# Order and layout of the q/k weight parts, the place of the Fourier channel products, and the last squares, in an encoder block

## The chip, the cores and the metric

The kernel runs on one core of a Trainium2 chip. The metric is the device time of one execution in microseconds (us), as the median of several runs. TensorE (PE) multiplies, VectorE (DVE) and ScalarE (ACT) work elementwise, GpSimd (POOL) does small elementwise steps, and DMA queues issued by SyncE (SP) and GpSimd bring the weights in.

## What is computed

One layer of an encoder on 256 positions of 2048 features. A combined projection gives q (12 heads of 128), k and v (4 heads each) and u (512 columns). Attention runs within a window of 128 positions; u goes through a two-dimensional Fourier transform, by groups of 128 channels, and a linear map for each group. Both results are normed, concatenated and projected; a gated feed-forward part with a short convolution and a final norm follow.

```python
def reference(x, norm1_g, w_in, sink, w_fourier, attn_out_g, fourier_out_g, w_out,
              norm2_g, w_up, dw_w, dw_b, w_down, normf_g):
    for _ in range(DEPTH):
        h = _rmsnorm(x, norm1_g)
        proj = h @ w_in
        ...
        a = _rmsnorm(_window_attention(q, k, v, sink), attn_out_g)
        f = _rmsnorm(_fourier_mix(u, w_fourier), fourier_out_g)
        x = x + jnp.concatenate([a, f], axis=-1) @ w_out
        x = x + _conv_ffn(_rmsnorm(x, norm2_g), w_up, dw_w, dw_b, w_down)
    return _rmsnorm(x, normf_g)

def _fourier_mix(u, w_fourier):
    B, S = u.shape[0], u.shape[1]
    ug = u.reshape(B, S, N_FOURIER_GROUPS, FOURIER_GROUP_DIM).astype(jnp.float32)
    f = jnp.real(jnp.fft.fft2(ug, axes=(1, 3), norm='ortho'))
    y = jnp.einsum('bsgc,gcd->bsgd', f.astype(u.dtype), w_fourier)
    return y.reshape(B, S, FOURIER_WIDTH)
```

## The kernel before

**Units and parts.** The work up to the output projection is a row of units, numbered by slot. Each unit has one weight tile of 128 x 2048 float32 numbers (1 MB), loaded by one DMA. Slots 4 to 7 are v, slots 8 to 23 the sixteen q and k heads in the order k0, q0, q1, q2, k1, q3 and so on, slots 24 to 31 the output projection. TensorE multiplies in a float32 format of less precision, so `split` (L168) makes two parts of each weight tile: ScalarE copies the raw tile into the high part (L174), and VectorE subtracts that from the raw tile for the low part (L175). A q/k unit is sixteen products of a high part with 512 columns (the high and the low half of the activations side by side, L362) and sixteen of a low part with 256 columns (L364). `still_weights` (L351) sets their order: with `lag` 0 a high and a low product alternate from the start, with `lag` 4 five high ones come first and five low ones last. `OPENING` (L49) gives lag 4 to the four k heads and to q1, q7 and q10; all others have 0. `parts_tile` (L156) hands out one of three buffers and places the high part at column 0 of it and the low part 16 columns past its middle ("still" in `PLACES`, L154).

**Order.** Nothing is scheduled by the framework: every engine runs its instructions in the order in which the program issues them. `unit` (L402) runs for slot i first the list `before[i]` (on TensorE, in front of the unit's products), then the products, then `beside[i]`, then `step`, which splits the weights of slot i + 2 and issues the load for slot i + 5, then `behind[i]`. `step` comes after `beside`, so on VectorE the low part of slot i + 2 stands behind the posts of slot i.

**A head's path.** With s the slot of a q head: the sum of its two halves and its own parts (`qk_out`, `qk_parts`) are issued beside s + 1, its scores on TensorE ahead of s + 2, `scores_out` on VectorE beside s + 2 (it adds the distances and finds the maxima, and writes the tile `sc`), `exps` on ScalarE behind s + 2, `weigh` on VectorE beside s + 3, the transposes of `sc` on TensorE (`turn`) ahead of s + 4, `turn_out` (the parts `pt`) beside s + 4, and the products with v (`values`) ahead of s + 5, with `values_out` beside it.

**The Fourier path.** `fourier_rows` and `fourier_rows_out` (slot 7) leave four tiles `uf0` to `uf3`. They carry the tag `sc`, as the score tiles do, and the tag has four buffers. `fourier_channels` (L547) multiplies `uf` of one group by the group's map, as full float32 products, ahead of slots 9 to 12. `fourier_channels_copy` (ScalarE, beside the same slot), `fourier_channels_join` (VectorE, behind it) and `fourier_channels_out` (beside the next slot) follow. The squares' total over the four groups (`total`) runs ahead of slot 14, its scale beside it. The buffers of a tag are given to a new tile when the last reader of an older one is through; the waits for that are put in with the build.

**The end.** The last columns of the down-projection, 512 for each of four column groups and two row blocks, come out in `last_product` (L1220). `last_post` (L1100) adds them to the residual on VectorE and squares the sum on ScalarE, with the row total in `ssq3`. The very last group, (3, 1), comes in two halves of 256 columns. `most_of` and `last_scale` (L1105, L1113) put the totals together on VectorE, GpSimd takes the power -0.5, and `finish` scales and stores the four column groups.

Of the kernel before, what the change touches and what calls it, by code (L numbers as in the profile page):

```python
# [8 lines left out]
F32 = mybir.dt.float32  # L9
F32R = mybir.dt.float32r  # L10
AF = mybir.ActivationFunctionType
ALU = mybir.AluOpType

P = 128
D = 2048
S = 256
NK = D // P
HD = 128
NH = 12
NKV = 4  # L20
GQA = 3
NG = 4
AW = NH * HD
FW = NG * P
DFF = 5504
NF = DFF // P
EPS = 1e-6
# [17 lines left out]
QK_ORDER = []  # L45
for _g in range(NKV):
    QK_ORDER += [("k", _g)] + [("q", _g * GQA + _i) for _i in range(GQA)]

OPENING = {("q", 1): 4, ("q", 7): 4, ("q", 10): 4}  # L49
OPENING.update({("k", g): 4 for g in range(NKV)})  # L50
N_U, N_V, N_QK = 0, 4, 8
N_OUT = N_QK + len(QK_ORDER)

# [43 lines left out]
def block_kernel(  # L97
# [18 lines left out]
    nc = tc.nc  # L116
    SL = slopes()
    ctx.enter_context(tc.manual_schedule())
    base = ctx.enter_context(tc.tile_pool(name="base", bufs=1))
    wp = ctx.enter_context(tc.tile_pool(name="wp", bufs=1))  # L120
# [4 lines left out]
    def f32(ap):  # L125
        return ap.bitcast(F32)
# [4 lines left out]


    units = [(None, 2048, "first")] * N_V
    units += [(w_in[i - N_V], 2048, "first" if i < N_QK else "still") for i in range(N_V, 24)]
    units += [(w_out[i], 2048, "moving") for i in range(16)]
    n_front = len(units)
    items, up_index = ff_items(), {}
# [17 lines left out]

    def parts_tile(name, place):  # L156
        t = wp.tile([P, 2 * 2048 + 128], F32R, tag="parts", name=name, bufs=3)
        oh, ol = PLACES[place]
        return t[:, oh : oh + 2048], t[:, 2048 + ol : 4096 + ol]

    def load(i):

        if i < len(units) - 1 and i not in raws:
            src, n, _ = units[i]
            raws[i] = wp.tile([P, 2048], F32, tag="raw", name=f"raw{i}", bufs=RAW)
            nc.sync.dma_start(raws[i][:, 0:n], src)

    def split(i):  # L168
        if i >= len(units):
            return  # L170
        _, n, place = units[i]
        raw = raws[i][:, 0:n]
        hi, lo = (t[:, 0:n] for t in parts_tile(f"parts{i}", place))
        nc.scalar.activation(hi, raw, AF.Copy)  # L174
        nc.vector.tensor_tensor(lo, raw, f32(hi), ALU.subtract)  # L175
        halves[i] = hi, lo
        load(i + RAW)
        load_more(i + RAW)
# [16 lines left out]
    xs = [base.tile([P, 2, 512], F32, tag=f"xs{c}", name=f"xs{c}") for c in range(4)]  # L195
# [10 lines left out]
    half_pow = base.tile([P, 2], F32, tag="half_pow", name="half_pow")  # L206
# [4 lines left out]
    ps = bank(dn, "ps_warm")  # L211
# [11 lines left out]
    for c in range(4):  # L223
        t = base.tile([P, 4, 512], F32R, tag=f"hT{c}", name=f"hT{c}")
# [36 lines left out]
    k = 0  # L261
# [89 lines left out]
    def still_weights(hi, lo, ps, kk, lag=0):  # L351


        todo = [("hi", k) for k in kk[: lag + 1]]
        for n, k in enumerate(kk):
            todo.append(("lo", k))
            todo += [("hi", q) for q in kk[lag + 1 + n : lag + 2 + n]]
        for part, k in todo:
            h = hT[k // 4][:, k % 4, :]
            s = slice(k * P, (k + 1) * P)  # L360
            if part == "hi":
                nc.tensor.matmul(ps, hi[:, s], h, start=k == 0, stop=False)  # L362
            else:
                nc.tensor.matmul(  # L364
                    ps[:, 0:S], lo[:, s], h[:, 0:S], start=False, stop=k == NK - 1
                )

    def still_thirds(hi, lo, ps):
# [24 lines left out]
    before, beside, behind = {}, {}, {}  # L393

    def at(when, i, f, *a):
        when.setdefault(i, []).append((f, a))
# [188 lines left out]
    at(beside, 8, lambda: rows_out(v_hi, v_lo, ps_v))  # L585
    at(behind, 8, distances)

    def fourier_channels_steps():
        for g in range(NG):
            i = 9 + g  # L590
            at(beside, i, fourier_channels_copy, g)
            at(behind, i, fourier_channels_join, g)
            at(beside, i + 1, fourier_channels_out, g)
        at(beside, 14, total_scale, "f", FW)


    ps_v = [bank(mm, f"ps_v{b}") for b in range(2)]
# [124 lines left out]
    for i in range(N_QK, N_OUT + 8):  # L722
        heads = {i - s: h for (kind, h), s in slot_of.items() if kind == "q"}
        new = [kh for kh, s in slot_of.items() if i - s == 1]
        if i - 9 in range(NG):
            at(before, i, fourier_channels, i - 9)
        if 5 in heads:
            at(before, i, values, heads[5])
        if 4 in heads:
            at(before, i, turn, heads[4])  # L730
        if i == 14:
            at(before, i, total, sq_f, "f")
        if 2 in heads:
            at(before, i, scores, heads[2])
        if 3 in heads:
            at(beside, i, weigh, heads[3])
        for kind, h in new:
            at(beside, i, lambda k=kind, h=h: qk_out(k, h, st.pop(("ps", k, h))))
        if 5 in heads:
            at(beside, i, values_out, heads[5])  # L740
        if 4 in heads:
            at(beside, i, turn_out, heads[4])
        for kind, h in new:
            at(beside, i, qk_parts, kind, h)
        if 2 in heads:
            at(beside, i, scores_out, heads[2])
            at(behind, i, exps, heads[2])

    fourier_channels_steps()
    for n, (kind, h) in enumerate(QK_ORDER):  # L750

        def work(hi, lo):
            ps = st["ps", kind, h] = bank(mm, f"ps_{kind}{h}")
            still_weights(hi, lo, ps, range(NK), lag=OPENING.get((kind, h), 0))

        unit(N_QK + n, work)

# [49 lines left out]
    for n, (c, kq) in enumerate(OUT_ORDER):  # L807
        i = N_OUT + n
# [14 lines left out]
        if kq >= 2:  # L823
            part = "a" if kq == 2 else "f"
            ps = ps_a[c] if kq < 3 else ps_a[c, "f"]
# [18 lines left out]
    parts = {}  # L844
# [242 lines left out]
    ssq3 = base.tile([P, 2, 5], F32, tag="ssq3", name="ssq3")  # L1087

    def square_sum(c, b, part, o, n):
        junk = wp.tile([P, 512], F32, tag="junk", name=f"junkc{c}{b}{part}")  # L1090
        nc.scalar.activation(
            junk[:, 0:n], xs[c][:, b, o : o + n], AF.Square,
            accum_out=ssq3[:, b, part : part + 1],
        )
# [5 lines left out]
    def last_post(c, b, ps, o=0, n=512, part=None):  # L1100

        add_scaled(xs[c][:, b, o : o + n], ps, b)
        square_sum(c, b, c if part is None else part, o, n)

    def most_of(b, n):  # L1105

        tot = base.tile([P, 1], F32, tag=f"tot3{b}", name=f"tot3{b}")
        nc.vector.tensor_reduce(tot, ssq3[:, b, 0:n], mybir.AxisListType.X, ALU.add)
        var = base.tile([P, 1], F32, tag=f"part3{b}", name=f"part3{b}")
        nc.vector.tensor_scalar(var, tot, 1.0 / D, EPS, ALU.mult, ALU.add)  # L1110
        return var

    def last_scale(b, n, var):  # L1113
        v = base.tile([P, 1], F32, tag=f"var3{b}", name=f"var3{b}")
        nc.vector.scalar_tensor_tensor(
            v, ssq3[:, b, n : n + 1], 1.0 / D, var, ALU.mult, ALU.add
        )
        r = base.tile([P, 1], F32, tag=f"rstd3{b}", name=f"rstd3{b}")
        nc.gpsimd.tensor_tensor(r, v, half_pow[:, 0:1], ALU.pow)
        return r  # L1120
# [17 lines left out]
    for q in range(2):  # L1138
        kind, j = items[q]
        ps = bank(mm, f"ps_{kind}{j}")  # L1140
# [16 lines left out]
    for n, it in enumerate(items):  # L1157
# [8 lines left out]
        if it[0] in ("gate", "val"):  # L1166
            kind, j = it
            ps = bank(mm, f"ps_{kind}{j}")
# [39 lines left out]
    i = up_index[n]  # L1208
# [11 lines left out]
    def last_product(c, b, o=0, n=512, part=None):  # L1220
        hi, lo = halves[i + c]
        ps = bank(dn, f"ps_e{c}{b}{o}")[:, 0:n]
        for q, k in enumerate(LAST):
            w = slice(q * 512 + o, q * 512 + o + n)
            ah, al = (act[k][:, p * S + b * P : p * S + (b + 1) * P] for p in range(2))
            end = q == len(LAST) - 1
            nc.tensor.matmul(ps, ah, hi[:, w], start=q == 0, stop=False)
            nc.tensor.matmul(ps, al, hi[:, w], start=False, stop=False)
            nc.tensor.matmul(ps, ah, lo[:, w], start=False, stop=end)
        if (c, b) == (0, 0):  # L1230
            ff_step(items.index(("last", 0)))
            split_last(3)
        last_post(c, b, ps, o, n, part)
        if c < 3:
            gain(c, b)
# [3 lines left out]
    r3 = last_scale(0, 3, most_of(0, 3))  # L1239
# [5 lines left out]
    for _ in outs:  # L1245
        pass
    last_product(2, 1)
    for p in range(2):
        last_product(3, 1, p * 256, 256, 3 + p)
    r3 = last_scale(1, 4, most_of(1, 4))  # L1250
    for _ in finish(1, r3, (2, 0, 3, 1)):
        pass

# [104 lines left out]
```

## Time and profile before

| | us |
|---|---|
| median of 3 runs | 946.41 |
| the runs | 946.23 to 946.63 |
| the profiled execution | 945.75 |
| its span | 944.0 |

The span is the time from the first to the last instruction of the program. The rows are read thus: in the time-ordered view, start, length, engine, line, operation, tiles and shapes, and in brackets the idle time of the engine before the row and what ended it. A row may hold several like instructions (x5); its length is then that of the group. A matmul's end is modelled and overlaps the next one's start, so the pace of TensorE is read from start to start. In the chain of waits a row has start, length, engine, tile, line and count. In the table of windows each engine has its busy time and, in brackets, its instructions; the number behind POOL's is the granted TensorE clock.

### The profile page before, as it was taken

To read this page: it belongs to the slowest core of one execution; us is meant where nothing else is said; L and a number is where in the kernel's file an instruction comes from. 1 tells how busy PE (TensorE), PEld (TensorE's weight loads), DVE (VectorE), ACT (ScalarE), POOL (GpSimd) and SP (SyncE) were. 2 spreads that over 40 slices of the span, in tenths; PEclk is the share of its full clock that TensorE was granted. 3 is DMA by queue.
4 is the path that set the end of the run, shared out by engine and by line. 5 is a ranking of instruction groups with operands and counts; after the bars stand their busy time and mean duration, and the time that the engine had idled before them with its cause. 6 is when DMAs were issued, how large, how long until landed. Compare 5 with 4: busy or idle time off the path is not lost.

```text
span 944.0 us, 15017 instructions
## 1 busy us (share of the span) xinstructions
PE 934.7 (99%) x6275; PEld 857.6 (91%) x6275; DVE 711.1 (75%) x817; ACT 536.6 (57%) x624; POOL 48.2 (5%) x64
## 2 busy tenths in 40 slices
PE   9999999999999999999999999999999999999996
PEld 8889998888888999999999999999999999999985
DVE  7568877666667766869776887768878678889695
ACT  7656766554454645446555565555555555655544
POOL 0000000000000000000000000000000000000003
PEclk9999999999999999999999999999999999999999
DMA  9864544456558677677798778787787978779742
GB/s 361 312 224 137 176 140 173 134 179 202 195 223 271 220 232 238 188 241 238 250 261 257 243 238 274 249 264 228 261 242 238 298 249 256 248 217 265 222 176 89
DMA packets 32628, 215.00 MB, mean 228 GB/s; under 512 B 3600, under 2 KB 3856, under 8 KB 8240
## 3 DMA queue, kind: packets, MB, share of 16 engines
q1 hardware_dynamic: 28448, 184.55, 53.7%
q0 software_dynamic: 4112, 29.49, 16.5%
q8 instruction: 49, 0.80, 0.3%
q14 instruction: 19, 0.16, 0.0%
HBM read 211.93 MB, written 2.10 MB: 227 GB/s over the span
## 4 chain that ended last, share of the span: by engine, by line
PE 99%; POOL 0%; ACT 0%; issue 0%; DVE 0%; ACTq 0%; POOLq 0%
PE ps_val L375 22%; PE ps_gate L375 21%; PE ps_q L362 5%; PE ps_P L1081 3%; PE ps_P L1080 3%; PE ps_P L1079 3%; PE ps_N L1080 3%; PE ps_N L1081 3%; PE ps_N L1079 3%; PE ps_q L364 2%; PE ps_u L257 2%; PE ps_a L347 2%; PE ps_a L345 2%; PE ps_a L346 2%; PE ps_gate L362 2%; PE ps_val L362 2%
## 5 line engine op out<-in xcount | busy, mean ns | idle before, releaser
L175 DVE TENSOR_TENSOR parts<-raw,parts 128x2048 fp32r<-128x2048 f32 (+1 forms) x129 | 293.5, 2275 | 72.9 <-ACT parts L174 72.8
L174 ACT ACTIVATE parts<-raw 128x2048 fp32r<-128x2048 f32 (+1 forms) x129 | 245.9, 1906 | 82.2 <-PE ps_gate L375 19.9
L375 PEld LDWEIGHTS ps_val<-hU,parts 128*128 128x128 f32 x1824 | 211.6, 188 | 2.2
L375 PE MATMUL ps_val<-hU,parts 128*128 128x256 f32 x1824 | 212.9, 276 | 0.0
L375 PEld LDWEIGHTS ps_gate<-hU,parts 128*128 128x128 f32 x1776 | 206.4, 188 | 2.5
L375 PE MATMUL ps_gate<-hU,parts 128*128 128x256 f32 x1776 | 207.3, 276 | 0.0
L362 PE MATMUL ps_q<-hT,parts 128*128 128x512 f32 x192 | 66.0, 395 | 0.0
L856 ACT ACTIVATE fa_v<-ps_val 128x256 f32<-128x256 f32 x38 | 14.6, 384 | 88.3 <-PE ps_val L375 88.2
L966 DVE TENSOR_TENSOR parts_N<-sumw,parts_N 128x2048 fp32r<-128x2048 f32 x18 | 41.2, 2291 | 21.2 <-ACT parts_N L965 21.1
L1079 PE MATMUL ps_P<-parts_P,op_P 128*128 128x512 f32 x144 | 56.0, 389 | 0.0
L1080 PE MATMUL ps_P<-parts_P,op_P 128*128 128x512 f32 x144 | 56.0, 389 | 0.0
L1081 PE MATMUL ps_P<-parts_P,op_P 128*128 128x512 f32 x144 | 56.0, 389 | 0.0
L364 PE MATMUL ps_q<-hT,parts 128*128 128x256 f32 x192 | 51.6, 279 | 0.0
L362 PEld LDWEIGHTS ps_q<-hT,parts 128*128 128x128 f32 x192 | 35.9, 188 | 7.4
L965 ACT ACTIVATE parts_N<-sumw 128x2048 fp32r<-128x2048 f32 x18 | 34.4, 1914 | 14.3 <-PE ps_gate L375 10.6
L1079 PE MATMUL ps_N<-parts_N,op_N 128*128 128x512 f32 x108 | 42.0, 389 | 0.0
L1080 PE MATMUL ps_N<-parts_N,op_N 128*128 128x512 f32 x108 | 42.0, 389 | 0.0
L1081 PE MATMUL ps_N<-parts_N,op_N 128*128 128x512 f32 x108 | 42.0, 389 | 0.0
L345 PE MATMUL ps_a<-parts,cat 128*128 128x512 f32 x96 | 37.9, 395 | 0.0
L347 PE MATMUL ps_a<-parts,cat 128*128 128x512 f32 x96 | 37.5, 391 | 0.0
L346 PE MATMUL ps_a<-parts,cat 128*128 128x512 f32 x96 | 37.3, 389 | 0.0
L364 PEld LDWEIGHTS ps_q<-hT,parts 128*128 128x128 f32 x192 | 35.4, 188 | 0.3
(350 smaller groups left out, 1513.1 us busy)
## 6 DMA issues: line engine op xcount, KB each, us to landing
raw<-in_w_up SPq DMA_DIRECT2D x86, 1024.0 KB, 5.6
raw<-in_w_in SPq DMA_DIRECT2D x20, 1024.0 KB, 6.4
sumw<-in_w_down POOLq DMA_DIRECT2D x18, 1024.0 KB, 8.5
raw<-in_w_out SPq DMA_DIRECT2D x16, 1024.0 KB, 4.8
raw<-in_w_down_late SPq DMA_DIRECT2D x4, 1024.0 KB, 6.2
u_raw<-in_u_in SPq DMA_DIRECT2D x5, 768.0 KB, 10.8
raw<-in_w_down_last SPq DMA_DIRECT2D x4, 768.0 KB, 4.4
xs<-in_x SPq DMA_DIRECT2D x4, 512.0 KB, 15.3
```

What stands on the lines that cost most here:

```text
L174: nc.scalar.activation(hi, raw, AF.Copy)
L175: nc.vector.tensor_tensor(lo, raw, f32(hi), ALU.subtract)
L345: nc.tensor.matmul(ps, ah, wh, start=first and q == q0, stop=False)
L346: nc.tensor.matmul(ps, al, wh, start=False, stop=False)
L347: nc.tensor.matmul(ps, ah, wl, start=False, stop=last and q == q0 + len(kk) - 1)
L362: nc.tensor.matmul(ps, hi[:, s], h, start=k == 0, stop=False)
L364: nc.tensor.matmul(ps[:, 0:S], lo[:, s], h[:, 0:S], start=False, stop=k == NK - 1)
L375: nc.tensor.matmul(ps[:, 0:S], w[:, s], h[:, o : o + S], start=k == 0 and n == 0, stop=k == NK - 1 and n == 2,)
L966: nc.vector.tensor_tensor(lo, src, f32(hi), ALU.subtract)
L1079: nc.tensor.matmul(ps, o[:, 0, p, :], hi[:, s], start=first and p == 0, stop=False)
L1080: nc.tensor.matmul(ps, o[:, 1, p, :], hi[:, s], start=False, stop=False)
L1081: nc.tensor.matmul(ps, o[:, 0, p, :], lo[:, s], start=False, stop=end)
```

## The change

Three things. First, every q/k unit has lag 7: eight high products, then eight times a low and a high one, then eight low ones. Its parts lie in four pieces of 1024 columns, the high ones at columns 16 and 1088 of the buffer and the low ones at 2128 and 3168; ScalarE's copy and VectorE's subtraction write them with one instruction each, as before. Second, the Fourier channel products of groups 0 to 3 stand ahead of slots 13, 14, 15 and 17, behind `values` and in front of `turn`; the squares' total and its scale move from slot 14 to slot 19. Third, the squares of the last 512 columns of the second row block are taken on VectorE with one multiplying reduction for each half; ScalarE adds up the other three totals with a scaled copy, and GpSimd's power reads the finished sum.

```diff
-OPENING = {("q", 1): 4, ("q", 7): 4, ("q", 10): 4}
-OPENING.update({("k", g): 4 for g in range(NKV)})
...
+        if place == "qk":
+
+            return [
+                t[:, o : o + 2 * n].rearrange("p (h f) -> p h f", h=2)[:, :, 0:1024]
+                for o, n in ((16, 1072), (2128, 1040))
+            ]
...
-        hi, lo = (t[:, 0:n] for t in parts_tile(f"parts{i}", place))
+        hi, lo = parts_tile(f"parts{i}", place)
+        if place == "qk":
+            raw = raw.rearrange("p (h f) -> p h f", h=2)
+        else:
+            hi, lo = hi[:, 0:n], lo[:, 0:n]
         nc.scalar.activation(hi, raw, AF.Copy)
         nc.vector.tensor_tensor(lo, raw, f32(hi), ALU.subtract)
...
+    CHANNELS_AT = (13, 14, 15, 17)
+
     def fourier_channels_steps():
-        for g in range(NG):
-            i = 9 + g
+        for g, i in enumerate(CHANNELS_AT):
             at(beside, i, fourier_channels_copy, g)
             at(behind, i, fourier_channels_join, g)
             at(beside, i + 1, fourier_channels_out, g)
-        at(beside, 14, total_scale, "f", FW)
+        at(beside, 19, total_scale, "f", FW)
...
-        if i - 9 in range(NG):
-            at(before, i, fourier_channels, i - 9)
         if 5 in heads:
             at(before, i, values, heads[5])
+        if i in CHANNELS_AT:
+            at(before, i, fourier_channels, CHANNELS_AT.index(i))
         if 4 in heads:
             at(before, i, turn, heads[4])
-        if i == 14:
+        if i == 19:
             at(before, i, total, sq_f, "f")
...
-            still_weights(hi, lo, ps, range(NK), lag=OPENING.get((kind, h), 0))
+            still_weights(hi, lo, ps, range(NK), lag=7)
...
-        square_sum(c, b, c if part is None else part, o, n)
+        if (c, b) != (3, 1):
+            square_sum(c, b, c if part is None else part, o, n)
...
+    sums3 = base.tile([P, 12], F32, tag="sums31", name="sums31")
+    most = base.tile([P, 3], F32, tag="most31", name="most31")
+    nc.scalar.activation(
+        most, ssq3[:, 1, 0:3], AF.Copy, scale=1.0 / D, accum_out=sums3[:, 0:1]
+    )
+    squares = wp.tile([P, 512], F32, tag="junk", name="junkc31")
     for p in range(2):
-        last_product(3, 1, p * 256, 256, 3 + p)
-    r3 = last_scale(1, 4, most_of(1, 4))
+        last_product(3, 1, p * 256, 256)
+        y = xs[3][:, 1, p * 256 : (p + 1) * 256]
+        nc.vector.tensor_tensor_reduce(
+            squares[:, p * 256 : (p + 1) * 256], y, y, 1.0 / D,
+            sums3[:, 0:1] if p else EPS, ALU.mult, ALU.add, sums3[:, p + 1 : p + 2],
+        )
+        if p == 0:
+            nc.vector.tensor_tensor(sums3[:, 0:1], sums3[:, 0:1], sums3[:, 1:2], ALU.add)
+    r3 = base.tile([P, 1], F32, tag="rstd31", name="rstd31")
+    nc.gpsimd.tensor_tensor(r3, sums3[:, 2:3], half_pow[:, 0:1], ALU.pow)
```

More of the change, by code (lines that the diff above doesn't have):

```diff
@@ L133, in block_kernel @@
     units = [(None, 2048, "first")] * N_V
-    units += [(w_in[i - N_V], 2048, "first" if i < N_QK else "still") for i in range(N_V, 24)]
+    units += [(w_in[i - N_V], 2048, "first" if i < N_QK else "qk") for i in range(N_V, 24)]
     units += [(w_out[i], 2048, "moving") for i in range(16)]
@@ L359, in still_weights @@
             h = hT[k // 4][:, k % 4, :]
-            s = slice(k * P, (k + 1) * P)
+            w = hi if part == "hi" else lo
+            if len(w.shape) == 3:
+                w = w[:, k // 8, k % 8 * P : (k % 8 + 1) * P]
+            else:
+                w = w[:, k * P : (k + 1) * P]
             if part == "hi":
-                nc.tensor.matmul(ps, hi[:, s], h, start=k == 0, stop=False)
+                nc.tensor.matmul(ps, w, h, start=k == 0, stop=False)
             else:
                 nc.tensor.matmul(
-                    ps[:, 0:S], lo[:, s], h[:, 0:S], start=False, stop=k == NK - 1
+                    ps[:, 0:S], w, h[:, 0:S], start=False, stop=k == NK - 1
                 )
```

## The prediction

> **What bounds the kernel now.** I read the page's busy table first, then its chain of waits, then the windows of the stretch that the change touches, then the time-ordered view of each engine there.
>
> ```profile
> PE 934.7 (99%) x6275; PEld 857.6 (91%) x6275; DVE 711.1 (75%) x817; ACT 536.6 (57%) x624; POOL 48.2 (5%) x64
> ...
> PE 99%; POOL 0%; ACT 0%; issue 0%; DVE 0%; ACTq 0%; POOLq 0%
> ...
> 53.19:162.09 108.90, 108.90 (x689) 98.27 (x688) 84.80 (x191) 71.83 (x139) 8.12 (x11) 1.00 0.48 163
> ```
>
> The last row is the stretch from the first q/k unit to the first product of the output projection: TensorE is busy for all of its 108.90 us, at full granted clock. So nobody keeps it waiting there, and only two things can move the end: a shorter stream of products, or a wait that appears. VectorE is busy for 84.80 us of the 108.90, ScalarE for 71.83; the slack is what covers their waits now.
>
> How long is the stream? In the chain of waits the small groups between the units have one length each, and the units differ:
>
> ```profile
> 58.10 0.76 PE L364 MATMUL ps_k<-hT,parts 128*128 128x256 f32 x5
> 58.69 0.60 PE L550 MATMUL ps_y<-uf,G 128*128 128x129 f32 x4
> 59.05 0.48 PE L362 MATMUL ps_q<-hT,parts 128*128 128x512 f32 x1
> 59.37 0.28 PE L364 MATMUL ps_q<-hT,parts 128*128 128x256 f32 x1
> ...
> 64.74 0.60 PE L550 MATMUL ps_y<-uf,G 128*128 128x129 f32 x4
> 65.10 1.41 PE L362 MATMUL ps_q<-hT,parts 128*128 128x512 f32 x5
> 66.34 0.28 PE L364 MATMUL ps_q<-hT,parts 128*128 128x256 f32 x1
> 66.46 0.39 PE L362 MATMUL ps_q<-hT,parts 128*128 128x512 f32 x1
> 66.68 0.28 PE L364 MATMUL ps_q<-hT,parts 128*128 128x256 f32 x1
> ...
> 84.23 0.44 PE ps_t L687 x4
> 84.67 0.71 PE ps_s L637 x6
> 90.83 0.71 PE ps_o L709 x6
> 91.98 0.34 PE ps_totf L485 x4
> ...
> 320.91 5.44 PE ps_val L375 x48
> ```
>
> The first q unit takes 64.74 - 59.05 = 5.69 us. The same number of columns in the feed-forward takes 5.44 (last row), the best pace this trace has. In the stretch stand eleven score groups and nine value groups of 0.71, nine transposes and four Fourier products of 0.44, and one total of 0.34: 20.3 us. That leaves 108.90 - 20.3 = 88.6 for sixteen units, 1.5 over 16 x 5.44 = 87.04.
>
> **The change, part by part.**
>
> *Eight high parts first, parts in four pieces.* The products are the same; only their order and the addresses of the weights change. ScalarE's copy and VectorE's subtraction keep 2048 elements each. From the rows: five low products in a row take (58.69 - 58.10) / 5 = 0.118 each, a pair of high and low at its better pace 66.68 - 66.34 = 0.34. A high product behind a Fourier group takes 59.37 - 59.05 = 0.32, where 66.68 - 66.46 = 0.22 is usual, so 0.1 belongs to the start; the run of five from 65.10 to 66.34 is then 0.23 each. Eight high, eight pairs and eight low in the old layout would be 8 x 0.23 + 8 x 0.34 + 8 x 0.118 = 5.50, and sixteen of them 88.1: a gain of 0.5. If the new offsets bring the pace of 5.44, the gain is 1.5. If instead every pair ran at the slow pace of the first q unit (5.69 less 0.1 for its start, over 16, is 0.35), a unit would be about 5.60 and the loss 1.0. No row shows these offsets, so the ends are -1.5 and +1.0; I take -0.7, nearer to the old layout's own rows than to the best pace, which only other shapes reach.
>
> *Fourier products beside transposes.* On TensorE nothing is gained to speak of: a Fourier group is 0.44 wherever it stands, and the slow first product behind it (those 0.32 for 0.22) is mostly the end of the group itself. I take 0, with 0.1 either way. The cost is elsewhere. The Fourier rows (`uf`, L547 to L550 read them) live in the four buffers of the tag `sc`, in which the scores' tiles live too. Before, product g stood at slots 9 to 12, so all were free when the scores needed them. Now they are read at slots 13, 14, 15 and 17. In the order of the changed program, with its waits, the first write of `sc0` on VectorE (slot 11) waits for the semaphore count that Fourier product 0 gives at the head of slot 13; `sc1` for the transposes of `sc0` in that same slot, since they share a buffer; `sc2` (slot 13) for product 1 at the head of slot 14. Queued behind `sc0` on VectorE are the low part of unit 13, the weighing of head 0, and the sum and low part of q2. TensorE needs head 0's weighed scores for the transposes that stand directly behind product 0, and q2 for the scores behind those. So everything between the two has lost its cover:
>
> ```profile
> 73.52 0.42 DVE L653 CUSTOM_DVE_ANT_0 sc<-ps_s,rel 128x256 f32<-128x256 f32 x1
> ...
> 74.88 0.48 DVE L218 SCALAR_TENSOR_TENSOR cat<-y,vec,cat 128x256 fp32r<-128x256 f32 x1
> 75.96 2.29 DVE L175 TENSOR_TENSOR parts<-raw,parts 128x2048 fp32r<-128x2048 f32 x1 [0.61 <-ACT parts L174]
> 78.17 0.28 DVE L563 TENSOR_TENSOR y<-yh 128x127 f32<-128x127 f32 x1
> ...
> 78.64 0.15 DVE L676 TENSOR_TENSOR sm<-sm,ex 128x2 f32<-128x2 f32 x1
> ...
> 79.56 0.42 DVE L616 TENSOR_TENSOR add_q<-ps_q,tmp_q 128x256 f32<-128x256 f32 x1
> 80.47 0.42 DVE L218 SCALAR_TENSOR_TENSOR qT<-add_q,qT 128x256 fp32r<-128x256 f32 x1 [0.48 <-ACT qT L217]
> ...
> 94.20 0.48 DVE L218 SCALAR_TENSOR_TENSOR cat<-ps_o,vec,cat 128x256 fp32r<-128x256 f32 x1
> 95.62 0.69 DVE L700 TENSOR_TENSOR pt<-ps_t,pt 128x512 fp32r<-128x512 f32 x1 [0.94 <-ACT pt L699]
> ```
>
> In slot 13, from the end of product 0: scores and their maxima 74.88 - 73.52 = 1.36; the low part 78.17 - 75.96 = 2.21 (ScalarE's exponentials run beside it); weighing 79.56 - 78.64 = 0.92; with 0.1 for the handovers TensorE idles 4.6. Then q2's sum and low part, 80.47 + 0.42 - 79.56 = 1.33, of which the transposes cover 0.44: 0.8 more with its handover. Slot 13 costs 5.4.
>
> What is late next: `sc2` starts at product 1, and behind it on VectorE, before the values of head 1 can run at the head of slot 15, stand 1.36, the low part 2.21, the join of Fourier group 0 (78.64 - 78.17 = 0.47), weighing 0.92, a sum 0.34, and from the `cat` part to the end of `pt` 95.62 + 0.69 - 94.20 = 2.11, in which ScalarE's square, waiting for that `cat`, holds its `pt` copy back. That is 7.4 against the transposes and one unit, 0.44 + 5.44 = 5.9 on TensorE: a stall of 1.5 at slot 15. The same list stands before the values of head 4 at slot 19, where the join of group 3 and a late `sc5` meet: 1.5 again. Slot 18 has it without the join, half covered: 0.6, an estimate from the same rows. From slot 20 no Fourier work is left and the covers of before return. Sum: 5.4 + 1.5 + 0.6 + 1.5 = 9.0; ends 5.4 (only the first) and 12 (each slot from 15 to 19 late by about a square's wait more).
>
> The moved steps issue no DMA; each slot's 1 MB load goes out after its low part, three units ahead, and a later TensorE only gives it more time. POOL's additions of the Fourier squares stay off the path, and the scale of the Fourier half, moved from slot 14 to 19, is first used in the output projection, past slot 24. TensorE's half-speed start is a rival below.
>
> *The last squares on VectorE.*
>
> ```profile
> 935.01 0.18 ACT L1091 ACTIVATION_READ_ACCUMULATOR junkc<-xs 128x1 f32 x1
> ...
> 935.72 0.48 DVE L865 SCALAR_TENSOR_TENSOR xs<-ps_e,rstd,xs 128x256 f32<-128x256 f32 x1 [0.55 <-PE ps_e L1229]
> ...
> 936.30 0.42 ACT L1091 ACTIVATE junkc<-xs 128x256 f32<-128x256 f32 x1 [0.52 <-DVE tot L1108]
> 936.62 0.19 ACT L1091 ACTIVATION_READ_ACCUMULATOR junkc<-xs 128x1 f32 x1
> 936.84 0.16 DVE L1115 SCALAR_TENSOR_TENSOR var<-ssq,part 128x1 f32<-128x1 f32 x1 [0.38 <-ACT junkc L1091]
> 937.08 0.55 POOL L1119 TENSOR_TENSOR rstd<-var,half_pow 128x1 f32<-128x1 f32 x1 [0.53 <-DVE var L1115]
> ```
>
> Now the sum ends at 935.72 + 0.48 = 936.20 and the power starts at 937.08. After: a reduction of 256 columns like L653 (0.42) and its accumulator, then one handover to POOL of 0.08: 936.8, a gain of 0.3. But VectorE must first add ScalarE's total of the other three columns, issued after the square that ends at 935.19 and itself an accumulating ScalarE step (at most the 0.42 and 0.19 of the rows above), and the sum of the last half stands behind it: up to 0.2 back. I take -0.2, ends -0.3 and +0.1.
>
> **The sum.** The profiled execution took 945.75 (span 944.0 and 1.75 around it), 0.66 below the median of 946.41. 945.75 - 0.7 + 0 + 9.0 - 0.2 = 953.85; with the 0.66, 954.5 as a median.
>
> **The rivals.**
>
> *TensorE falls back to its starting speed.* At the head of the span:
>
> ```profile
> 0.99 4.37 PE L213 MATMUL ps_warm<-ones 128*128 128x128 f32 x20 [0.99 <-POOL ones L205]
> ```
>
> Twenty passes of 128 columns in 4.37 us are 0.22 each; four in a transpose group take 0.44, 0.11 each. So TensorE starts at half speed and stays there some four microseconds. If the 4.6 us of idling in slot 13 bring that back, about 4.2 us run at half speed: +2.1, 956.6. Against it: this trace has no second gap to show it. The Trainium skill, "TensorE: Matmul & The Clock Gate", Part 1, says that a whole idle window of about 3.4 us halves the clock and that the windows run freely; the half-speed start agrees with it, and by it a gap of 4.6 would hold such a window about one time in three.
>
> *Only the first stall costs.* If the later slots keep their covers, 3.6 less: 950.9. For it: VectorE has 24 us idle in the 108.90. Against it: the list of slot 15 is longer than the unit beside it.
>
> *The layout goes the wrong way.* Units of 5.60: 1.7 more than in the sum, 956.2. For it: the pairs change pace from unit to unit already.
>
> *The other side: the wait is hidden.* In the trace, `sc0` is weighed at 79.56, 4.7 us before its transposes at 84.23. If the buffers came free early enough for that lead to cover the wait, only the gains would be left: 946.41 - 1.5 - 0.2 = 944.7, faster. It decides if product 0 ends five microseconds ahead of the transposes; it stands directly before them, so this needs the changed program to wait otherwise than its semaphores say.
>
> **How the numbers follow.** Forecast 0.60, half speed 0.20, first stall only 0.10, layout 0.05, hidden 0.05. The forecast's own range is 951.5 to 957 (the ends of the stall partly used). The range of all is 950.2 to 958.5. What a measurement can tell from no change is 0.2%, 1.9 us. Faster 0.04, same 0.02, slower 0.94: the hidden wait gives the first two, all else is slower by over 4 us.
>
> **What would show it.** Right: TensorE idle for 4 to 5 us between the first Fourier product and the first transposes, ended by VectorE's weighing; then about 1.5 before the values of head 1; no waits from slot 20 on; units of 5.4 to 5.5; the last power about 0.6 us after the last sum of the residual instead of 0.88. Wrong: no idle TensorE in slot 13, or idle time in the unit products themselves, which would make the low parts or the loads the cause; or a granted clock under 1.00 behind the gap, which would be the half-speed rival.

## The result, and the profile after

| | before | after |
|---|---|---|
| median | 946.48 us (4 runs) | 957.86 us (4 runs, 956.86 to 958.09) |
| profiled execution | 945.75 | 958.08 |
| its span | 944.0 | 956.3 |
| first q/k unit starts at | 53.19 | 53.42 |
| first product of the output projection at | 162.09 | 173.37 |

After over before is 1.0118, with a 95% interval from 1.0106 to 1.0130: slower. The two stretches of the span after the first unit's start hold nearly all of the 12.3 us: 173.37 - 53.42 = 119.95 against 108.90, and from there to the end 956.3 - 173.37 = 782.93 against 944.0 - 162.09 = 781.91.

The table of windows of the changed kernel, first for the stretch from the first unit to the output projection, then for four windows of 3.4 us around the moved Fourier product. The columns are the window, its length, each engine's busy time, the granted clock, the DMA share and GB/s:

```profile
53.42:173.37 119.95, 113.57 (x689) 100.89 (x688) 83.42 (x190) 70.20 (x139) 10.41 (x11) 0.97 0.43 147
...
82.87:86.28 3.41, 0.06 (x1) 0.00 (x0) 3.25 (x7) 1.73 (x6) 0.00 (x0) 1.00 0.00 0
86.28:89.70 3.42, 2.50 (x11) 2.25 (x12) 2.80 (x13) 2.02 (x2) 0.00 (x0) 0.50 0.70 216
89.70:93.12 3.42, 3.42 (x10) 2.65 (x10) 3.12 (x7) 2.31 (x8) 0.00 (x0) 0.50 0.22 91
93.12:96.53 3.41, 3.41 (x23) 3.10 (x22) 1.72 (x5) 2.50 (x3) 0.00 (x0) 1.00 0.91 312
```

TensorE is busy for 113.57 of the 119.95 us, and the clock is 0.97. Before, it was busy for all of the stretch at 1.00. The four windows show two of the losses in one place: almost nothing to do from 82.87 to 86.28 (the 0.06 us is the end of the Fourier product), then half the clock from 86.28 to 93.12, although the work is back at 87.20.

TensorE in order of time there, then ahead of the values of slots 15, 18 and 19, with the untouched group of slot 16 at 113.14 between them:

```profile
81.38 1.10 PE L375 MATMUL ps_k<-hT,parts 128*128 128x256 f32 x8
82.32 0.61 PE L561 MATMUL ps_y<-uf,G 128*128 128x129 f32 x4
87.20 1.09 PE L699 MATMUL ps_t<-ident,sc 128*128 128x128 f32 x4 [4.28 <-DVE sc L692]
...
89.63 3.61 PE L373 MATMUL ps_q<-hT,parts 128*128 128x512 f32 x8
...
102.92 1.10 PE L375 MATMUL ps_q<-hT,parts 128*128 128x256 f32 x8
104.63 0.38 PE L721 MATMUL ps_o<-pt,v_hi 128*128 128x256 f32 x1 [0.60 <-ACT pt L711]
105.35 0.38 PE L721 MATMUL ps_o<-pt,v_hi 128*128 128x256 f32 x1 [0.34 <-DVE pt L712]
...
106.05 0.27 PE L561 MATMUL ps_y<-uf,G 128*128 128x129 f32 x1
...
113.14 0.40 PE L721 MATMUL ps_o<-pt,v_hi 128*128 128x256 f32 x2
...
113.85 0.87 PE L649 MATMUL ps_s<-kT,qT 128*128 128x256 f32 x6
...
127.30 0.28 PE L721 MATMUL ps_o<-pt,v_hi 128*128 128x256 f32 x1
...
128.56 0.60 PE L699 MATMUL ps_t<-ident,sc 128*128 128x128 f32 x4
...
133.56 1.11 PE L375 MATMUL ps_q<-hT,parts 128*128 128x256 f32 x8
135.19 0.38 PE L721 MATMUL ps_o<-pt,v_hi 128*128 128x256 f32 x1 [0.53 <-ACT pt L711]
...
136.61 0.60 PE L699 MATMUL ps_t<-ident,sc 128*128 128x128 f32 x4
```

The transposes wait 4.28 us, and VectorE's weighing of `sc` ends the wait. Read from start to start, later waits are larger than the idle time in the brackets, since a matmul's modelled end covers part of them. Eight low products take 82.32 - 81.38 = 0.94; ahead of slots 15 and 19 they take 1.71 and 1.63. A values group takes 113.85 - 113.14 = 0.71; at slots 15, 18 and 19 it takes 1.42, 1.26 and 1.42. The eight high products at 89.63 take 3.4 us, where at full clock they take 1.85 (shown below): that is the half clock.

VectorE in slot 13 of the changed kernel, and the first write of `sc2`, later:

```profile
82.96 0.42 DVE L665 CUSTOM_DVE_ANT_0 sc<-ps_s,rel 128x256 f32<-128x256 f32 x1 [11.00 <-PE ps_y L561]
...
86.70 0.62 DVE L692 TENSOR_SCALAR sc<-sc,ex 128x256 f32<-128x256 f32 x2
...
98.12 0.42 DVE L665 CUSTOM_DVE_ANT_0 sc<-ps_s,rel 128x256 f32<-128x256 f32 x1 [3.24 <-PE ps_y L561]
```

VectorE stands idle for 11.00 us until the Fourier product has read `uf0`, and then runs, one after the other, all that TensorE is waiting for. The bracket names the last reader of the buffer; before the change the same row stood at 73.52 with no wait.

The end of the changed kernel, VectorE and then GpSimd:

```profile
946.60 1.51 DVE L1271 CUSTOM_DVE_ANT_0 junkc<-xs 128x256 f32<-128x256 f32 x1
...
948.29 0.48 DVE L877 SCALAR_TENSOR_TENSOR xs<-ps_e,rstd,xs 128x256 f32<-128x256 f32 x1
948.81 0.48 DVE L1271 CUSTOM_DVE_ANT_0 junkc<-xs,sums 128x256 f32<-128x256 f32 x1
```

```profile
946.56 1.27 POOL L1110 TENSOR_TENSOR xs<-xs,gfb 128x512 f32<-128x512 f32 x1 [0.46 <-ACT junkc L1103]
949.38 0.56 POOL L1278 TENSOR_TENSOR rstd<-sums,half_pow 128x1 f32<-128x1 f32 x1 [1.55 <-DVE sums L1271]
```

The first reduction takes 1.51 us, the second, of the same shape, 0.48. GpSimd's gain runs from 946.56 to 947.83, and the long reduction ends 0.28 after it. The addition of the last half (948.29) stands behind that reduction. The power does come 948.77 to 949.38, 0.6 us, after the end of that addition, as foretold; but the addition itself is late.

### The profile page after: what moved, and what is told of

Its sections match the earlier page's. It is cut to its first block, busy times and chain, and to the rows that moved or that the text cites. A ratio compares the mean times of both kernels' runs of the same rounds, so it can differ in the third digit from the quotient of the medians.

```text
span 956.3 us, 15009 instructions
## 1 busy us (share of the span) xinstructions
PE 939.5 (98%) x6275; PEld 860.0 (90%) x6275; DVE 712.2 (74%) x819; ACT 534.4 (56%) x622; POOL 50.4 (5%) x64
## 4 chain that ended last, share of the span: by engine, by line
PE 93%; DVE 3%; ACT 2%; DMA 1%; issue 1%; SPq 0%; POOL 0%; ACTq 0%; POOLq 0%
PE ps_val L386 22%; PE ps_gate L386 21%; PE ps_P L1093 3%; PE ps_P L1092 3%; PE ps_P L1091 3%; PE ps_q L373 3%; PE ps_N L1091 3%; PE ps_N L1093 3%; PE ps_N L1092 3%; PE ps_a L354 2%; PE ps_a L352 2%; PE ps_a L353 2%; PE ps_gate L373 2%; PE ps_val L373 2%; PE ps_q L375 2%; PE ps_u L264 1%
## 5 line engine op out<-in xcount | busy, mean ns | idle before, releaser
L373 PE MATMUL ps_q<-hT,parts 128*128 128x512 f32 x192 | 58.8, 402 | 0.0
L373 PEld LDWEIGHTS ps_q<-hT,parts 128*128 128x128 f32 x192 | 36.3, 194 | 7.3
L375 PE MATMUL ps_q<-hT,parts 128*128 128x256 f32 x192 | 39.9, 279 | 0.0
L978 DVE TENSOR_TENSOR parts_P<-sumw,parts_P 128x2048 fp32r<-128x2048 f32 x9 | 20.6, 2290 | 16.6 <-ACT parts_P L977 16.6
```

What stands on the lines that cost most here:

```text
L373: nc.tensor.matmul(ps, w, h, start=k == 0, stop=False)
L375: nc.tensor.matmul(ps[:, 0:S], w, h[:, 0:S], start=False, stop=k == NK - 1)
L978: nc.vector.tensor_tensor(lo, src, f32(hi), ALU.subtract)
```

## The experiments

The theory after these readings: the loss is three things. Waits for the buffers that `uf` shares with the scores (about 8.8 us), TensorE at half speed behind the longest of them (about 2.1), and VectorE held by GpSimd in the end (about 1). The layout of the parts gains nothing. The rivals: the moved products or the layout cost time themselves, the half clock costs nothing that the waits would not, and the long reduction is long by itself.

Three pieces of each profiled execution, from the time-ordered view and the span, separate these:

| kernel | median us | over before (95%) | first unit at | to the output projection | from there to the end |
|---|---|---|---|---|---|
| before | 946.48 | | 53.19 | 108.90 | 781.91 |
| after | 957.86 | 1.0118 (1.0106 to 1.0130) | 53.42 | 119.95 | 782.93 |
| own buffers for `uf` | 947.37 | 1.0015 (1.0005 to 1.0024) | 53.44 | 109.05 | 782.91 |
| Fourier products back | 947.60 | 1.0015 (1.0006 to 1.0025) | 53.76 | 109.27 | 782.97 |
| TensorE kept busy | 956.25 | 1.0108 (1.0093 to 1.0123) | 53.80 | 117.84 | 782.96 |
| only the last squares | 947.09 | 1.0010 (1.0001 to 1.0020) | 53.12 | 108.90 | 782.88 |
| squares, gain off GpSimd | 946.49 | 1.0004 (0.9995 to 1.0014) | 53.93 | 108.90 | 782.07 |
| old layout, lag 7 | 945.89 | 0.9998 (0.9989 to 1.0007) | 53.64 | 108.78 | 781.88 |
| thirds | 947.01 | 1.0010 (1.0002 to 1.0019) | 54.04 | 109.50 | 781.96 |
| thirds and tail | 947.18 | 1.0011 (1.0002 to 1.0020) | 53.26 | 109.50 | 782.14 |
| both faults repaired | 946.59 | 1.0004 (0.9996 to 1.0013) | 53.40 | 109.04 | 782.06 |
| a shorter gap | 957.87 | 1.0119 (1.0103 to 1.0134) | 53.94 | 119.34 | 782.92 |

The kernel before, timed beside the experiments, had medians of 946.11 to 946.19, and the ratios go by these runs (that of the changed kernel by 946.48). The first unit's start wanders between 53.1 and 54.0, in kernels that do not differ there, and why was not worked out. So the start is kept apart from the other two columns, which repeat to 0.1 us where the kernels do not differ.

**Own buffers for the Fourier rows.** The changed kernel, with `uf` in the tag `cat`:

```diff
-            t = ph.tile([P, 512], F32, tag="sc", name=f"uf{g}", bufs=4)[:, 0:S]
+            t = cat_pool.tile([P, 512], F32, tag="cat", name=f"uf{g}")[:, 0:S]
```

> The changed kernel, but the four Fourier row tiles lie in buffers of their own (tag cat) instead of the scores' tag sc; products, places and order are the changed kernel's. Theory (the wait for the shared buffer, and what follows it): no idle TensorE in slot 13, none at slots 15, 18 and 19, granted clock 1.00 throughout; only the longer end (+1.0) stays, so about 947.5 us. Rival (VectorE and ScalarE have too much to do in slots 13 to 19 wherever the buffers are): the first gap goes, but 3 to 4 us of stalls at slots 15 to 19 stay, about 951. Rival (the layout slows the units): the waits go, but the units are still longer than before, over 949.

The stretch falls from 119.95 to 109.05. Its row in the table of windows, then TensorE and VectorE around the same product, in order of time:

```profile
53.44:162.49 109.05, 109.05 (x690) 98.39 (x689) 84.50 (x191) 71.87 (x139) 10.44 (x11) 1.00 0.48 162
```

```profile
82.33 0.61 PE L561 MATMUL ps_y<-uf,G 128*128 128x129 f32 x4
82.78 0.60 PE L699 MATMUL ps_t<-ident,sc 128*128 128x128 f32 x4
83.13 0.95 PE L649 MATMUL ps_s<-kT,qT 128*128 128x256 f32 x6
83.93 1.31 PE L373 MATMUL ps_q<-hT,parts 128*128 128x512 f32 x5
```

```profile
78.08 0.42 DVE L665 CUSTOM_DVE_ANT_0 sc<-ps_s,rel 128x256 f32<-128x256 f32 x1
...
82.14 0.61 DVE L692 TENSOR_SCALAR sc<-sc,ex 128x256 f32<-128x256 f32 x2
```

The scores are written at 78.08, ahead of the Fourier product, the weighing ends at 82.75, and TensorE has no gap. So the shared buffers are the cause of the waits, and by them of the half clock: 119.95 - 109.05 = 10.90 us. The later position of the products, by itself, costs nothing.

**The Fourier products back in their old places,** with the layout and the last squares as changed:

```diff
-    CHANNELS_AT = (13, 14, 15, 17)
+    CHANNELS_AT = (9, 10, 11, 12)
...
-        at(beside, 19, total_scale, "f", FW)
+        at(beside, 14, total_scale, "f", FW)
...
```

> The changed kernel with the Fourier products back ahead of slots 9 to 12 and their total at 14; layout, lag 7 and the last squares as changed. Theory: 947.5 us, as with buffers of their own, since the place alone costs nothing: the two differ by under 0.5. Rival (a place beside the transposes is worth something by itself): this one is slower than the one with own buffers by about 0.4, four times the 0.09 of a slow first product.

No gap either, and 109.27: 0.37 over before, for the layout with its lag. The kernel with own buffers is 0.22 shorter, so the later places save a little, half of the 0.4 that the rival gave them. A unit of this kernel in order of time shows that the new layout does not bring the pace of 5.44:

```profile
72.35 2.01 PE L373 MATMUL ps_q<-hT,parts 128*128 128x512 f32 x8
74.20 0.28 PE L375 MATMUL ps_q<-hT,parts 128*128 128x256 f32 x1
74.32 0.40 PE L373 MATMUL ps_q<-hT,parts 128*128 128x512 f32 x1
...
74.67 0.40 PE L373 MATMUL ps_q<-hT,parts 128*128 128x512 f32 x1
...
77.00 1.10 PE L375 MATMUL ps_q<-hT,parts 128*128 128x256 f32 x8
77.94 0.61 PE L561 MATMUL ps_y<-uf,G 128*128 128x129 f32 x4
```

The eight high ones take (74.20 - 72.35) / 8 = 0.231 each, the low ones (77.94 - 77.00) / 8 = 0.118, as reckoned; but a pair takes 74.67 - 74.32 = 0.35, not 0.34, and the unit 77.94 - 72.35 = 5.59.

**TensorE kept busy.** The changed kernel, with 18 products of ones by ones behind Fourier product 0, into columns of its bank that nobody reads (the trace counts two passes for each):

```diff
+    def keep_busy():
+        for _ in range(18):
+            nc.tensor.matmul(held["y", 0][:, S : S + P], ones, ones, start=True, stop=True)
...
+        if i == CHANNELS_AT[0]:
+            at(before, i, keep_busy)
```

> The changed kernel with 18 products of a tile of ones more, ahead of slot 13 behind the first Fourier product, into columns that nobody reads: about 3.9 us of work at full pace that fills the gap. Theory (the gap halves TensorE's clock): granted clock 1.00 throughout, transposes, scores and q3 of slot 13 back to 0.44, 0.8 and 5.5, about 2.5 us faster than the changed kernel, 955.3. Rival (their slow pace comes from late parts or buffers): no change, 957.9 or a little more.

The row of windows of its stretch, then TensorE in order of time:

```profile
53.80:171.64 117.84, 115.28 (x725) 102.87 (x724) 83.84 (x191) 70.20 (x139) 10.41 (x11) 1.00 0.45 153
```

```profile
83.14 4.18 PE L569 MATMUL ps_y<-ones 128*128 128x128 f32 x36
87.58 0.72 PE L703 MATMUL ps_t<-ident,sc 128*128 128x128 f32 x4 [0.26 <-DVE sc L696]
88.53 1.19 PE L653 MATMUL ps_s<-kT,qT 128*128 128x256 f32 x6 [0.23 <-ACT qT L224]
89.56 1.99 PE L373 MATMUL ps_q<-hT,parts 128*128 128x512 f32 x8
```

The clock stays at 1.00 and the same waits remain: the transposes start 87.58 - 83.14 = 4.44 us after the first of the extra products, about as long as the changed kernel's gap. The stretch is 119.95 - 117.84 = 2.11 shorter, where 2.5 was expected; the median falls by 1.6 only, since the first unit starts 0.38 later. The 2.11 are the price of the half clock by itself; the waits are 117.84 - 109.05 = 8.79. At full clock the wait for q2 can also be read: transposes to scores 88.53 - 87.58 = 0.95, against 83.13 - 82.78 = 0.35 with own buffers, and scores to unit 1.03 against 0.80.

**Only the last squares:** the kernel before with the third edit alone (its diff is that of the change).

> The kernel before with the third part of the change alone (last 512 columns squared on VectorE). Theory (VectorE's reduction with two operands in SBUF stands still while GpSimd multiplies the gain into (2,1)): the first reduction takes 1.5 us, the power starts 1.0 us later than before, 947.4 us. Rival (the prediction's term): the reduction takes 0.4 to 0.5 and the kernel gains 0.2, 946.2. Rival (the first reduction is long because it is the first of its kind): 1.5 too, told apart by the run that takes the gain off GpSimd.

The stretch is that of before, and the end 0.97 longer. VectorE and GpSimd:

```profile
935.24 1.51 DVE L1258 CUSTOM_DVE_ANT_0 junkc<-xs 128x256 f32<-128x256 f32 x1
```

```profile
935.20 1.27 POOL L1098 TENSOR_TENSOR xs<-xs,gfb 128x512 f32<-128x512 f32 x1 [0.73 <-ACT junkc L1091]
```

The same pair of rows as in the changed kernel, so the third edit loses by itself.

**The same without the GpSimd step.** The gain of group (2, 1) is multiplied later, in `finish` on VectorE:

```diff
-        if c < 3:
+        if c < 3 and (c, b) != (2, 1):
             gain(c, b)
...
-            if c == 3:
-                gf = gfb[:, 1536:2048]
+            if c == 3 or (c, b) == (2, 1):
+                gf = gfb[:, c * 512 : (c + 1) * 512]
```

> The kernel before with the last squares on VectorE, and with the gain of (2,1) taken off GpSimd: finish multiplies it in on VectorE together with the scale, as it does for the fourth column group. Theory (the lock between GpSimd's gain and VectorE's reduction): the first reduction takes 0.4 to 0.5 instead of 1.5, the power starts 1.2 us earlier than with the last squares alone and 0.3 earlier than before; 0.2 is given back by the longer scale, so 946.1, 1.0 faster than with the last squares alone. Rival (the first reduction of its kind is slow): 1.5 stays and the time is 947.1 or more.

```profile
936.05 0.43 DVE L1258 CUSTOM_DVE_ANT_0 junkc<-xs 128x256 f32<-128x256 f32 x1
...
936.66 0.48 DVE L865 SCALAR_TENSOR_TENSOR xs<-ps_e,rstd,xs 128x256 f32<-128x256 f32 x1
```

On VectorE the first reduction, still the first of its kind, now takes 0.43, and the end is 0.81 shorter than with GpSimd beside it: the long reduction came from GpSimd's step. The end is still 0.16 longer than before, so the expected 946.1 was missed by 0.4. Counted from the first unit's start, which is 0.74 later here, the addition of the last half begins 0.20 later than before (936.66 against 935.72), behind the first half's reduction. The power begins only 0.07 earlier (937.75 against 937.08) and not 0.3. And the two columns that `finish` scales on VectorE take 1.41 us instead of 1.14, since both now carry the gain.

**The old layout with lag 7:** the kernel before with `lag=7` in place of `OPENING`.

> The kernel before with lag 7 in every q/k unit and nothing else: the old places, parts in two pieces. Theory (pace goes with how a unit starts, not with the four pieces): the stretch of the q/k units is within 0.5 us of the 108.90 of before and of the 109.27 of the changed layout with the Fourier products where they were; time 946.0 to 946.8. Rival (the pieces are worth something over lag 7 in the old layout): the stretch is 109.8 or more.

108.78 against 108.90: the order is worth 0.1 us, and its ratio of 0.9998 (0.9989 to 1.0007) cannot be told from no change. The four pieces (109.27 with the same order and places) are 0.5 worse than the old two.

**Thirds.** Here q and k units use an order and a layout that the kernel has for the feed-forward part (`still_thirds`, "thirds"): three products of 256 columns for each weight block, all added up in one half of the bank, so that the sum of the two halves falls away. The second version adds the last squares without the GpSimd step. The cut below leaves out the new places of the parts and the sum that falls away.

```diff
-            still_weights(hi, lo, ps, range(NK), lag=OPENING.get((kind, h), 0))
+            still_thirds(hi, lo, ps)
...
```

> The kernel before with the feed-forward's order in the q/k units: 48 products of 256 columns (high weights with the high half, high with the low half, low with the high half) into one sum, parts in the feed-forward's places; the sum of two halves after each unit falls away. In the feed-forward this order ran at 5.44 us for a unit whatever stood before. Theory (what the q/k units lose is lost to runs and pairs of unequal products that do not settle): units of 5.44 to 5.50, stretch 107.6, time 945.1. Rival (the loss comes from the score and value groups between the units): units as before, 946.2.

> The two together: thirds in the q/k units, the last squares on VectorE, the gain of (2,1) off GpSimd. If both act as told they add up: 945.0, 1.2 under the kernel before. If the parts do not add, about 946.

The stretch is 109.50 in both, 0.6 longer than before. Units took from 5.45 to 5.79 instead of 5.44 throughout: some do not reach the pace that the feed-forward has, and why is open. It was a try at a better kernel, and a miss: 945.1 and 945.0 were expected.

**Both faults repaired:** the changed kernel with `uf` in its own buffers and the gain of (2, 1) off GpSimd.

> The changed kernel with the Fourier rows in the tag cat (no shared buffer with the scores) and without the GpSimd gain of group (2, 1), which finish multiplies on VectorE. All three edits stay. If the shared buffers and the GpSimd step beside the first reduction are the whole loss, its span is that of before plus 0.15 for the stretch of the units, plus 0.2 for the end piece: 944.0 + 0.35 = 944.4, give or take 0.3 for the start, and the median 946.2 to 946.8. Rival: the two repairs disturb each other or the edits cost something of their own that the single runs hid; then it is above 947.2.

109.04 and 782.06: within 0.15 of before in both pieces, and 1.0004 (0.9996 to 1.0013) over it. All three edits are in this kernel, so of the 12.3 us at most 0.3 are left for the edits themselves.

**A shorter gap.** The kernel kept busy, with three products of ones by ones instead of 18; TensorE's idle time ahead of the transposes is then 3.60 us.

> The changed kernel with 3 products of ones by ones behind Fourier product 0 (six passes of 128 columns, about 0.7 us), into columns of its bank that nobody reads: TensorE's idle time ahead of the first transposes falls from 4.3 to about 3.6 us, which is still over the 3.35 us after which the clock fell in the changed kernel (86.28 less the end of product 0 at 82.93). Theory A, the clock falls a set time after the last product: half speed in every run, mean clock 0.993 to 0.994, span 956 to 956.3, no gain over the changed kernel. Theory B, the clock is judged in windows of about 3.4 us that run freely: a gap of 3.6 holds a whole window in few runs (0.2 / 3.4, about one in twenty), so nearly all runs keep the full clock, mean 0.996 to 0.998, span 954.2 to 954.8 as with the kernel kept busy.

The median is 957.87, but one of its four runs took 956.28 with a clock of 0.996; the other three took 957.79 to 957.97 with 0.993 to 0.994. The windows of the profiled one, a run with the lower clock:

```profile
82.07:85.48 3.41, 2.04 (x18) 1.85 (x17) 1.93 (x7) 0.67 (x3) 0.00 (x0) 1.00 0.00 0
85.48:88.89 3.41, 0.94 (x6) 0.68 (x6) 2.86 (x7) 1.75 (x7) 0.00 (x0) 1.00 0.27 55
88.89:92.30 3.41, 3.41 (x12) 2.79 (x12) 3.11 (x8) 3.41 (x8) 0.00 (x0) 0.50 0.60 252
92.30:95.71 3.41, 3.41 (x20) 2.98 (x19) 2.98 (x9) 1.45 (x4) 0.00 (x0) 1.00 0.52 175
```

Both theories miss. The clock falls at 88.89, which is 4.78 us and not 3.35 after the last product (it ended at 84.11), so A is out. And it fell in three runs of four, where B as put allowed one in twenty. The half speed lasted one window here and two in the changed kernel, so the stretch is 0.61 shorter than there, and 119.34 - 117.84 = 1.50 over the kernel kept busy. The first unit starts 0.52 later, so the median is that of the changed kernel.

What fits both records is a window of 3.41 us that judges the next one, without having to be wholly idle. The edges of the windows are counted back in steps of 3.41 from the times at which the clock changes. 0.94 us of work in 3.41 lost the clock here, 2.04 kept it, and a full window brought it back. In the changed kernel, 0.06 lost it and 2.50 at half speed did not bring it back, which is why half speed lasted two windows there and one here.

Every trace has one case more, at its end, when TensorE has no work left. The same kernel there:

```profile
945.63:949.04 3.41, 1.24 (x11) 1.04 (x10) 2.88 (x6) 1.02 (x4) 1.65 (x2) 1.00 0.40 154
949.05:952.46 3.41, 0.00 (x0) 0.00 (x0) 1.30 (x4) 1.33 (x2) 0.55 (x1) 0.50 0.36 138
```

Here 1.24 us of work lost the clock, 2.18 us after the last product. In the kernel before, the window from 933.38 has 2.30 us of work and the next one, without any, is still at full clock; the clock falls behind that, at 940.21, 4.53 us after the last product. So it is no set time after the last product, and the share of work below which a window loses the clock lies between 1.24 and 2.04 us of 3.41; where in between was not tried.

An estimate from these figures: a gap of 4.28 us, in the worst place split evenly over two windows, leaves 3.41 - 2.14 = 1.27 us of work in each, hardly more than what lost the clock. One of 3.60 leaves 1.61 and may keep it. That agrees with four runs of four at half speed in the changed kernel and three of four here.

## Why the prediction was right, and where it was not

The forecast was 954.5 us; 957.86 was measured, above the forecast's own range (951.5 to 957) and inside the range with the rivals (950.2 to 958.5). The main mechanism and its price were right; a rival came in on top, and two small terms were wrong. By the forecast's terms, in the profiled executions:

| term | forecast | measured | from |
|---|---|---|---|
| waits for the shared buffers | +9.0 | +8.79 | kept busy less own buffers |
| half speed behind the gap | a rival, +2.1 | +2.11 | after less kept busy |
| layout and lag, places | -0.7 + 0 | +0.15 | own buffers less before |
| the last squares | -0.2 | +1.02 | end piece of after less before |
| start of the first unit, which wanders | none | +0.23 | 53.42 less 53.19 |
| sum | +8.1 | +12.30 | span 956.3 less 944.0 |

**The waits were right, slot by slot.** From start to start: slot 13 has 87.20 - 82.32 - 0.45 = 4.43 idle (4.6 foretold) and, from the kernel kept busy, 0.60 + 0.23 for q2 (0.8; the forecast's own rows give 1.33 - 0.44 = 0.89); slot 15 has 1.71 - 0.94 and 1.42 - 0.71, together 1.5 (1.5); slot 18 0.55 (0.6); slot 19 0.69 + 0.71 = 1.4 (1.5). The step that carried it was not a time but a reader: which instruction last reads the buffer that VectorE writes next, and how much stands behind that write. No wait follows from slot 20 on, where each values group takes 0.71 again. The rival of the first stall only is refuted by the rows at slots 15 to 19, the hidden wait by the 4.28.

**The half-speed rival came in, at its price.** Its chance of 0.20 was what failed. It rested on whether a gap of 4.6 us holds a whole idle window, about one time in three; all four runs of the changed kernel have a clock of 0.993 or 0.994, and even the gap of 3.60 lost it in three runs of four. The Trainium skill, "TensorE: Matmul & The Clock Gate", Part 1, has the window's length right (3.4 us; 3.41 here), and that the clock comes back after a busy one agrees too. That the window must be an idle one does not: the record shows windows with 0.94 and 1.24 us of work that lost the clock. That the price fits is in part luck: the rival reckoned with 4.2 us at half speed, and the trace has 6.84, of which 0.92 pass before the transposes start. And the forecast held against the rival that the trace of before has no second gap, but its end shows the clock falling, at 940.21.

**The layout was mis-sized.** The step that failed is the pair: 0.34 was taken from one q unit as the better pace, and the new layout was given a further gain. The pairs ran at 0.34 or 0.35 with both layouts, and in place of -0.7 the term measured +0.15 with the later places and +0.37 without: the wrong sign, but inside its ends of -1.5 and +1.0. The units of the layout rival came (5.59, it had 5.60), but not its loss of 1.0, since the units of before ran from 5.44 to 5.69 already. Why a unit takes the one pace or the other is open.

**The last squares have the wrong sign, outside their ends.** The forecast priced the reduction at 0.42, by L653, which reads PSUM and one SBUF tile, and looked for what VectorE would have to wait for by semaphores. It did not look at GpSimd's column, although a gain ran beside the place. Without that gain the term measured +0.16, still not -0.2. The trace of before shows the mechanism in a small step, L657 on VectorE. Here stand one of its rows with GpSimd at work and one without, in order of time, and then GpSimd's own rows, the last of them the gain beside the end:

```profile
74.33 0.38 DVE L657 TENSOR_TENSOR neg<-mx,rq_neg 128x2 f32<-128x2 f32 x1
...
103.49 0.16 DVE L657 TENSOR_TENSOR neg<-mx,rq_neg 128x2 f32<-128x2 f32 x1
```

```profile
73.94 0.74 POOL L478 TENSOR_TENSOR sq_f<-sq_f,sq 128x256 f32<-128x256 f32 x1 [24.83 <-ACT sq L477]
...
935.27 1.27 POOL L1098 TENSOR_TENSOR xs<-xs,gfb 128x512 f32<-128x512 f32 x1 [0.73 <-ACT junkc L1091]
```

The row at 74.33 ends with GpSimd's step (74.71 and 74.68) and takes 0.38; the free one takes 0.16. L653, with its one SBUF input, takes 0.42 at 73.87 too, beside the same GpSimd step. The Trainium skill, "SBUF — State Buffer", section "SBUF: two separate sides", states the rule: VectorE and GpSimd share a pair of SBUF ports under an exclusive lock, and a VectorE operation with two SBUF inputs against a GpSimd operation that reads SBUF is held until the other is through. The traces agree: the square's operand is given twice, as two SBUF inputs, and 1.51 fell to 0.43 when GpSimd had nothing to do. The residual addition, which reads PSUM and SBUF, kept its 0.48 beside the gain of before (935.72 to 936.20, the gain from 935.27 to 936.54).

## What to carry to other kernels

When a reader is moved later, look up who writes its buffer next, and count everything queued behind that writer on its engine; here a private buffer for four small tiles took away 10.9 us that no product's own length showed. A gap on TensorE, here of 3.6 or 4.3 us, can be paid a second time behind its end, by one or two windows of 3.41 us at half speed (1.5 and 2.1 us here). Before an operation with two SBUF inputs goes to VectorE, look at what GpSimd does in that microsecond.

## What was not expected of the hardware

The granted clock changed in steps of 3.41 us, and even a window with 36% of work (1.24 of 3.41) lost it. At full clock, one with 60% kept it (2.04); at half speed, one with 73% did not restore it (2.50 of 3.42). VectorE's wait for GpSimd appears in no bracket and in no releaser: it shows only as a longer row, 1.51 for 0.48, so it has to be looked for by comparing rows of one shape.
